# Two up-projection chunks in one tile, with 512-column products

## The chip, the cores and the metric

The kernel runs on one core of one Trainium2 chip. The metric is the device time of one execution in microseconds, as the median over runs; smaller is better. Beside it stands one profiled execution, whose span (first to last instruction of the program) is a little shorter than its time.

## The reference

One decoder layer on 256 tokens of width 1024, in float32:

```python
mix = hybrid_mixer(x, ...)                      # mLSTM branch and attention branch, gated, summed, projected
x = layer_norm(ALPHA * x + mix, ln1_g, ln1_b)
u = causal_dwconv(jnp.einsum("bsd,df->bsf", x, w_up), conv_ffn)     # w_up: 1024 x 5632
g, up = jnp.split(u, 2, axis=-1)
ffn = jnp.einsum("bsf,fd->bsd", jax.nn.silu(g) * up, w_down)        # w_down: 2816 x 1024
x = layer_norm(ALPHA * x + ffn, ln2_g, ln2_b)
```

The convolution is depthwise over three token positions. The change lies in the first columns of `w_up`.

## The kernel before, in words

Every float32 operand of a product is split into a high part (rounded to the matmul's float32r form) and a low part (the rest). A product of two such operands is three matmuls on TensorE, high by high, high by low and low by high, added up in PSUM (`mm3`, lines 125 to 127). The contraction over 1024 runs over eight slices of 128 rows (`KT` = 8, index k). One operand of a matmul is stationary (128 by 128, loaded before it), the other moves through (256 columns in nearly all of the kernel).

The weights come from HBM in a stream of 1 MB chunks in a fixed order (`chunk_order`): first projection, four groups of mixer projections, branch projections `wa` and `wb`, output projection `wo` (four chunks), and then up chunks (`up` 0 to 21) interleaved with down chunks (`dn`). One step of the main loop handles one chunk: it loads the chunk five places ahead (`load`, on the queue of SyncE), splits the chunk two places ahead into high and low parts (`split_parts`: a cast on ScalarE, line 91, and a subtraction on VectorE, line 92, in two halves), and then issues the step's matmuls (`step_up` and the like). Each engine runs its instructions in the order in which the program issues them.

An up chunk holds 128 columns of the gate half and 128 of the other half of `w_up`, so 256 columns. From chunk 2 on, the weights are stationary and all 256 tokens move (`mm_feat`), which gives features by tokens, as the convolution wants it. Chunks 0 and 1 are done the other way round (`mm_tok`): 128 tokens of the normalized activations are stationary and 256 weight columns move. So they can start on token half 0 while half 1 is still in the first layer norm. Their order is:

- step `up` 0: products of token half 0 for k = 0 to 6, both chunks at each k; four transposes of half 1 (`x1_transpose(1, 0)`, tile `ps_t`); products for k = 7; four more transposes of half 1; `x1_split` of both (tiles `x1h` and `x1l`);
- step `up` 1: products of token half 1, k = 0 to 7, both chunks at each k;
- then the results are copied to SBUF (`copy`, tile `tu`, on ScalarE), and transposed back in the middle of step `up` 2 (`back`, eight transposes, tile `ps_upT`).

Step `up` 2 takes its first stationary operand from a copy of it, `wfirst`. The split weights of chunks 0 and 1 do not lie in the stream's buffers but in four tiles of a pool of their own, `aheadh0`, `aheadl0`, `aheadh1` and `aheadl1`, filled during the steps `wo` 0 and `wo` 1.

Many tiles are allocated some words larger than needed, and used from an offset on. So the position in SBUF of a product's moving rows, relative to its stationary rows, is set by hand; the function `shift` does it for the stream's chunks:

```python
    if kind in ("vm", "vb", "o"):
        return 48
    if kind in ("wa", "wb"):
        return 56
    return 0 if kind in ("wo", "dn") else 16
```

The results of chunk j were accumulated in one PSUM bank per chunk (`ps_up`, 128 by 2 by 256: token half, column).

Of the kernel before, what the change touches and what calls it, by code (L numbers as in the profile page):

```python
# [11 lines left out]
F32R = mybir.dt.float32r  # L12
# [6 lines left out]
P = 128  # L19
S = 256  # L20
D = 1024
KT = D // P
# [47 lines left out]
class Kernel:  # L70
# [101 lines left out]
    def run(self):  # L172
# [28 lines left out]
        for part, a, b in (("x", 0, 1), ("w", 0, 1), ("x", 1, 4), ("w", 1, 2), ("w", 2, 4), ("x", 4, 8), ("w", 4, 6),  # L201
# [3 lines left out]
            else:  # L205
                s, c = cut[a][0], slice(cut[a][1].start, cut[b - 1][1].stop)
# [110 lines left out]
        first = {k: self.order.index((k, 0)) for k in ("wa", "wo", "up")}  # L317
        for s, (kind, i) in enumerate(self.order):
            if s == 8:
                self.elem_work(s, self.split_parts(s + 2))  # L320
                pre_cm.__exit__(None, None, None)
                self.open_att(att_cm.__enter__())
            if s == first["wa"]:
                self.elem_work(s)
                att_cm.__exit__(None, None, None)
                mix_cm.__exit__(None, None, None)
                self.open_post(post_cm.__enter__())
                mg = mg_cm.__enter__()
                self.mgh = mg.tile([P, KT, S], F32R, name="mgh")
                self.mgl = mg.tile([P, KT, S], F32R, name="mgl")  # L330
            if s == first["wo"]:
                self.elem_work(s)
                y_cm.__exit__(None, None, None)
                zp = ahead_cm.__enter__()
                for j in range(2):
                    self.extra[first["up"] + j] = tuple(
                        zp.tile([P, 2112], F32R, name=f"ahead{n}{j}")[:, 8:8 + 2048] for n in "hl")
            if s == first["up"]:
                self.elem_work(s)
                mg_cm.__exit__(None, None, None)  # L340
                self.fp = ffn_cm.__enter__()
            late = s == first["up"]
            self.elem_work(s, [] if late or s == 8 else self.split_parts(s + 2))
            self.load(s + 5)
            if s in (first["wo"], first["wo"] + 1):
                self.split(s + 4)
            getattr(self, "step_" + kind)(s, i, bo)
            for f in self.side_pe.pop(s, []):
                f()
            if late:  # L350

                self.wfirst = self.fp.tile([P, P + 64], F32R, name="wfirst")[:, 48:48 + P]
                nc.scalar.copy(self.wfirst, self.raw[s + 2][:, 0:P])
                self.split(s + 2)
# [602 lines left out]
    def step_up(self, s, i, *a):  # L957
        if i == 0:

            self.hid = {}  # L960
            self.pt_up = [self.ps_side([P, 2, S], f"ps_up{j}") for j in range(2)]
        if i < 2:
            for k in range(KT):
                if i == 0 and k == KT - 1:
                    self.x1_transpose(1, 0)
                for j in range(2):
                    self.mm_tok(self.w[s - i + j], [self.pt_up[j][:, t, :] for t in range(2)], self.x1h, self.x1l,
                                toks=(i,), ks=(k,))
            if i == 0:
                def trans():  # L970
                    self.x1_transpose(1, 1)
                    for h in range(2):
                        self.x1_split(1, h)
                self.side_pe.setdefault(s, []).append(trans)
                return
            del self.w[s - 1], self.w[s]
            tu = self.fp.tile([P, 2, 2, S], F32, name="tu")

            def copy():
                for j in range(2):  # L980
                    self.nc.scalar.copy(tu[:, j], self.pt_up[j])

            def back():
                for j in range(2):
                    ps = self.ps_side([P, 2, S], f"ps_upT{j}")
                    for f in range(2):
                        for t in range(2):
                            self.nc.tensor.transpose(ps[:, f, t * P:(t + 1) * P], tu[:, j, t, f * P:(f + 1) * P],
                                                     self.ident)
                    self.pt_up[j] = ps  # L990
            self.evac[s] = copy
            self.back = back
            self.up_parts = [self.up_evac(j, lambda j=j: self.pt_up[j]) for j in range(2)]
            return
        ps = self.ps_main(f"ps_up{i}")
        self.mm_feat(s, ps, self.x1h, self.x1l, *(self.back, self.wfirst) if i == 2 else ())
        conv, gate = self.up_evac(i, lambda: ps)
        parts = [conv, None, None, gate]
        if i == 2:
            (a0, b0), (a1, b1) = self.up_parts  # L1000
            parts = [a0, a1, conv, b0, None, None, b1, gate]
        self.evac[s] = parts
# [187 lines left out]
```

## Time and profile before

| | |
|---|---|
| median of 3 runs | 490.8 us (490.51 to 491.31) |
| profiled execution | 490.16 us, span 488.4 us |
| mean granted TensorE clock in it | 0.994 |
| TensorE busy | 477.0 us (98%) |
| VectorE busy | 369.3 us (76%) |
| ScalarE busy | 286.2 us (59%) |
| GpSimd busy | 30.6 us (6%) |
| moved by DMA | 93.77 MB, mean 192 GB/s |

A matmul's busy time counts it from start to modelled end, and successive matmuls overlap in the array. What TensorE gets through is therefore read from the starts of successive matmuls. "PEld" is the loading of the stationary operand, which goes on beside matmuls. The steps `up` 0 and `up` 1 run from 296.77 to 309.07 us of the span.

### The profile page before, as it was taken

To read this page: it belongs to the slowest core of one execution; us is meant where nothing else is said; L and a number is where in the kernel's file an instruction comes from. 1 tells how busy PE (TensorE), PEld (TensorE's weight loads), DVE (VectorE), ACT (ScalarE), POOL (GpSimd) and SP (SyncE) were. 2 spreads that over 40 slices of the span, in tenths; PEclk is the share of its full clock that TensorE was granted. 3 is DMA by queue.
4 is the path that set the end of the run, shared out by engine and by line. 5 is a ranking of instruction groups with operands and counts; after the bars stand their busy time and mean duration, and the time that the engine had idled before them with its cause. 6 is when DMAs were issued, how large, how long until landed. Compare 5 with 4: busy or idle time off the path is not lost.

```text
span 488.4 us, 9811 instructions
## 1 busy us (share of the span) xinstructions
PE 477.0 (98%) x4070; PEld 470.0 (96%) x4070; DVE 369.3 (76%) x659; ACT 286.2 (59%) x476; POOL 30.6 (6%) x46
## 2 busy tenths in 40 slices
PE   8999999999999999999999999999999999999992
PEld 4999999999999999999999999999999999999992
DVE  4967995788588858886677788988668766876886
ACT  5857767495658666856655622767456545654620
POOL 0600011001100110001000001000000000000001
PEclk9999999999999999999999999999999999999997
DMA  8984565555555645543964491827465556454202
GB/s 281 376 299 122 210 196 205 178 180 188 181 191 174 189 160 197 201 150 116 368 231 172 174 344 42 302 89 258 173 236 165 205 173 224 176 204 173 87 2 86
DMA packets 17886, 93.77 MB, mean 192 GB/s; under 512 B 4497, under 2 KB 4889, under 8 KB 7857
## 3 DMA queue, kind: packets, MB, share of 16 engines
q1 hardware_dynamic: 13682, 87.08, 50.1%
q0 software_dynamic: 4160, 6.07, 4.1%
q8 instruction: 32, 0.52, 0.4%
q14 instruction: 12, 0.10, 0.1%
HBM read 92.05 MB, written 2.63 MB: 194 GB/s over the span
## 4 chain that ended last, share of the span: by engine, by line
PE 97%; DMA 1%; DVE 1%; SPq 0%; ACT 0%; issue 0%; POOL 0%; POOLq 0%
PE ps_up L127 8%; PE ps_up L125 8%; PE ps_up L126 8%; PE ffn L127 4%; PE ffn L126 4%; PE ffn L125 4%; PE ps_vm L125 2%; PE ps_qm L125 2%; PE ps_vm L126 2%; PE ps_vm L127 2%; PE ps_ga L125 2%; PE ps_ga L127 2%; PE ps_vb L125 2%; PE ps_vb L126 2%; PE ps_vb L127 2%; PE ps_ga L126 2%
## 5 line engine op out<-in xcount | busy, mean ns | idle before, releaser
L92 DVE TENSOR_TENSOR wl<-raw,wh 128x1024 fp32r<-128x1024 f32 (+1 forms) x162 | 187.7, 1199 | 25.3 <-ACT wh L91 25.2
L91 ACT CAST wh<-raw 128x1024 fp32r<-128x1024 f32 (+1 forms) x162 | 158.4, 1030 | 8.6 <-DMA raw<-in_wst_dram 5.9
L127 PE MATMUL ps_up<-x1h,wl 128*128 128x256 f32 x320 | 88.5, 277 | 0.0
L126 PE MATMUL ps_up<-x1l,wh 128*128 128x256 f32 x320 | 88.5, 276 | 0.0
L125 PE MATMUL ps_up<-x1h,wh 128*128 128x256 f32 x319 | 88.3, 277 | 0.0
L126 PEld LDWEIGHTS ps_up<-x1l,wh 128*128 128x128 f32 x320 | 60.2, 188 | 0.0
L127 PEld LDWEIGHTS ps_up<-x1h,wl 128*128 128x128 f32 x320 | 60.1, 188 | 0.0
L125 PEld LDWEIGHTS ps_up<-x1h,wh 128*128 128x128 f32 x319 | 59.9, 188 | 0.0
L1020 DVE SCALAR_TENSOR_TENSOR cu<-ps_up,vec,cu 128x255 f32<-128x255 f32 (+1 forms) x80 | 33.1, 476 | 23.1 <-ACT cu L1016 23.0
L127 PE MATMUL ffn<-wh,hl 128*128 128x256 f32 (+1 forms) x170 | 47.7, 281 | 0.0
L126 PE MATMUL ffn<-wl,hh 128*128 128x256 f32 (+1 forms) x170 | 47.7, 281 | 0.0
L125 PE MATMUL ffn<-wh,hh 128*128 128x256 f32 (+1 forms) x170 | 47.7, 281 | 0.0
L91 ACT CAST hh<-cu 128x256 fp32r<-128x256 f32 x22 | 8.9, 407 | 42.9 <-DVE cu L1028 42.9
L126 PEld LDWEIGHTS ffn<-wl,hh 128*128 128x128 f32 x170 | 32.0, 188 | 0.3
L125 PEld LDWEIGHTS ffn<-wh,hh 128*128 128x128 f32 x170 | 31.9, 188 | 0.3
L127 PEld LDWEIGHTS ffn<-wh,hl 128*128 128x128 f32 x170 | 31.9, 188 | 0.3
L1016 ACT ACTIVATE cu<-ps_up,vec 128x256 f32<-128x256 f32 x40 | 16.7, 469 | 25.7 <-PE ps_up L127 25.7
L125 PE MATMUL ps_gb<-xth,wh 128*128 128x256 f32 x64 | 18.0, 282 | 0.0
L126 PE MATMUL ps_vm<-wl,xth 128*128 128x256 f32 x64 | 17.9, 280 | 0.0
L127 PE MATMUL ps_vm<-wh,xtl 128*128 128x256 f32 x64 | 17.9, 280 | 0.0
L927 POOL TENSOR_TENSOR rs<-rs,mhalf 128x1 f32<-128x1 f32 x4 | 2.7, 666 | 242.4 <-DVE rs L926 242.4
L125 PE MATMUL mix<-wh,mgh 128*128 128x256 f32 x64 | 17.8, 279 | 0.0
(295 smaller groups left out, 1441.7 us busy)
## 6 DMA issues: line engine op xcount, KB each, us to landing
raw<-in_wst_dram SPq DMA_DIRECT2D x78, 1024.0 KB, 4.9
raw<-in_wst_dram SPq DMA_DIRECT2D x5, 512.0 KB, 8.0
lnrow<-in_rows_dram POOLq DMA_DIRECT2D x4, 512.0 KB, 6.8
band<-table POOLq DMA_DIRECT2D x4, 384.0 KB, 12.2
toe<-band POOLq DMA_DIRECT2D x4, 256.0 KB, 4.4
xtok<-in_x_dram POOLq DMA_DIRECT2D x1, 1024.0 KB, 7.7
out_dram<-r SPq DMA_DIRECT2D x3, 256.0 KB, 2.0
raw<-in_wst_dram SPq DMA_DIRECT2D x2, 256.0 KB, 3.8
```

Source lines behind the costliest of these rows:

```text
L91: self.nc.scalar.copy(wh, raw)
L92: self.nc.vector.tensor_sub(wl, raw, wh.bitcast(F32))
L125: mm(ps, ah if first is None else first, bh, start=start, stop=False)
L126: mm(ps, ah, bl, start=False, stop=False)
L127: mm(ps, al, bh, start=False, stop=stop)
L927: nc.gpsimd.tensor_tensor(st["rs"], st["rs"], self.mhalf[:, 0:1], op=ALU.pow)
L1016: act.activation(cu[:, j, :], ps[:, j, :], AF.Copy, scale=tap(2, j))
L1020: v.scalar_tensor_tensor(cu[:, j, o:], ps[:, j, :S - o], tap(t, j), cu[:, j, o:], op0=ALU.mult, op1=ALU.add)
```

## The change

The four tiles become two, one of the high and one of the low parts, each with both chunks one behind the other. They are used from offset 24 words on instead of 8. At each k a token half's products take the columns of both chunks in one matmul: 512 columns, in two runs of 256 that lie 2048 words apart. The steps issue 48 matmuls of 512 columns instead of 96 of 256. A PSUM bank holds the results of one token half for both chunks instead of one chunk for both halves. The copies to `tu` go by token half accordingly; the layout of `tu` and the transposes behind it are as they were.

```diff
                 zp = ahead_cm.__enter__()
+                self.pair = [zp.tile([P, 4160], F32R, name="ahead" + n)[:, 24:24 + 4096] for n in "hl"]
                 for j in range(2):
-                    self.extra[first["up"] + j] = tuple(
-                        zp.tile([P, 2112], F32R, name=f"ahead{n}{j}")[:, 8:8 + 2048] for n in "hl")
+                    self.extra[first["up"] + j] = tuple(t[:, j * 2048:(j + 1) * 2048] for t in self.pair)
...
-            self.pt_up = [self.ps_side([P, 2, S], f"ps_up{j}") for j in range(2)]
+            self.pt_up = [self.ps_side([P, 2, S], f"ps_up0{t}") for t in range(2)]
         if i < 2:
+            wh, wl = (t.rearrange("p (j k f) -> p j k f", j=2, k=KT) for t in self.pair)
+            c = slice(i * P, (i + 1) * P)
             for k in range(KT):
                 if i == 0 and k == KT - 1:
                     self.x1_transpose(1, 0)
-                for j in range(2):
-                    self.mm_tok(self.w[s - i + j], [self.pt_up[j][:, t, :] for t in range(2)], self.x1h, self.x1l,
-                                toks=(i,), ks=(k,))
+                self.mm3(self.pt_up[i], self.x1h[:, k, c], self.x1l[:, k, c], wh[:, :, k, :], wl[:, :, k, :], k == 0,
+                         k == KT - 1)
...
             def copy():
-                for j in range(2):
-                    self.nc.scalar.copy(tu[:, j], self.pt_up[j])
+                for t in range(2):
+                    self.nc.scalar.copy(tu[:, :, t, :], self.pt_up[t])
```

## The prediction

> **What bounds the kernel now.** I read the page first, then the waits of the whole span, then the timelines of TensorE, ScalarE and VectorE around the changed steps.
>
> ```profile
> span 488.4 us, 9811 instructions
> PE 477.0 (98%) x4070; PEld 470.0 (96%) x4070; DVE 369.3 (76%) x659; ACT 286.2 (59%) x476; POOL 30.6 (6%) x46
> PE 97%; DMA 1%; DVE 1%; SPq 0%; ACT 0%; issue 0%; POOL 0%; POOLq 0%
> ```
>
> TensorE is busy 98% of the span, and the chain that ended last is 97% TensorE. The waits of TensorE are two of 1.2 us at the start, and one of its weight loads in the changed steps:
>
> ```profile
> PE ps_o L159 <- ACT wh L91: 1.2, 1, 1.2
> PE warm_ps L194 <- DVE warm L191: 1.2, 1, 1.2
> ...
> PEld ps_up L127 <- DVE x1l L92: 0.2, 1, 0.2
> ```
>
> So what the change is worth is what it does to the intervals between starts of products on TensorE, and nothing else. (A product's own duration in the trace, 276 ns, overlaps its successor's and is of no use.) The timeline of TensorE over the two changed steps, columns start and duration:
>
> ```profile
> 296.77 0.28 PE L125 MATMUL ps_up<-aheadh,x1h 128*128 128x256 f32 x1
> ...
> 301.60 0.28 PE L127 MATMUL ps_up<-aheadh,x1l 128*128 128x256 f32 x1
> 301.73 0.60 PE L947 MATMUL ps_t<-ident,x 128*128 128x128 f32 x4
> 302.08 0.37 PE L125 MATMUL ps_up<-aheadh,x1h 128*128 128x256 f32 x1
> ...
> 302.86 0.60 PE L947 MATMUL ps_t<-ident,x 128*128 128x128 f32 x4
> 303.21 0.36 PE L125 MATMUL ps_up<-aheadh,x1h 128*128 128x256 f32 x1
> 303.42 0.28 PE L126 MATMUL ps_up<-aheadl,x1h 128*128 128x256 f32 x1
> 303.73 0.39 PE L127 MATMUL ps_up<-aheadh,x1l 128*128 128x256 f32 x1
> ...
> 304.31 0.28 PE L125 MATMUL ps_up<-aheadh,x1h 128*128 128x256 f32 x1
> ...
> 309.07 0.28 PE L125 MATMUL ps_up<-x1h,wfirst 128*128 128x256 f32 x1
> ```
>
> The reader is to see two rhythms of the same instruction. Token half 0 has 42 products up to the first transposes: (301.73 − 296.77)/42 = 118 ns each. Half 1 has 42 from 304.31 on: (309.07 − 304.31)/42 = 113.3 ns each. It isn't the clock:
>
> ```profile
> core 0: us, PE busy (x), PEclk, DMA share, GB/s
> 296.77:301.73 4.96, 4.96 (x45) 1.00 0.02 3
> 304.31:309.07 4.76, 4.76 (x44) 1.00 0.54 177
> ```
>
> Full clock in both, and DMA nearly idle in the slower one. I call them the slow and the fast rhythm (+4.5 ns for each product).
>
> **What a 512-column product costs.** Two places have them: the first projection, and the first and last hidden chunk of the down projection.
>
> ```profile
> 9.27 0.39 PE L159 MATMUL ps_o<-wh,xth 128*128 128x512 f32 x1
> ...
> 17.20 0.39 PE L159 MATMUL ps_o0b<-wl,xth 128*128 128x512 f32 x1
> 321.25 0.39 PE L125 MATMUL ffn<-wh,hh 128*128 128x512 f32 x1
> ...
> 323.35 0.28 PE L125 MATMUL ffn<-wh,hh 128*128 128x256 f32 x1
> ```
>
> In the first, 35 intervals take 17.20 − 9.27 = 7.93 us: 226.6 ns, twice the fast 113.3. In the second, nine take 2.10 us: 233.3 ns. What differs in the program is the distance (first byte of the moving rows less first byte of the stationary rows, modulo 256). From the addresses that the allocator gives in the kernel before: in the first projection (43,072 − 95,296) it is 0; in `ffn`, and in nearly all 256-column products, 192. The changed steps have 192 now: 195,552 + 32 for `aheadh0`, less 119,872 for `x1h`. After, worked out by hand: two tiles of 16,640 bytes end where the four ended (229,344), so the rows begin at 196,064 + 96 = 196,160; less 119,872 that is 298 × 256, distance 0. For the low tile, 212,800, also 0. The text of the change holds, and I take 226.6; 233.3 is the upper end if distance isn't what parts the two places. The moving operand now has two runs of 256 columns 8 KB apart; no row has such an operand. Two separate products have two runs as well: 2 × 113.3 bounds it from below, no row of 512 columns being faster, and 2 × 118 from above. I take the lower end, which is what the contiguous 512 columns cost at this distance.
>
> The Trainium skill (TensorE: Matmul & The Clock Gate, Step-by-step: what each phase is for) gives TensorE two independent read ports, so that loading the next weights takes nothing from the running product. By that rule distance would not matter and the two places would show one interval; they show 226.6 and 233.3 ns, which speaks against it here, though the places differ in more than distance. By the rule the pair's 48 products would cost one interval between those two, whatever the pad, and the saving would lie between 0.20 and 0.52.
>
> **The change part by part.** The path now, from the rows above: 42 products 4.96; transposes 0.35; six products 0.78; transposes 0.35; six products with the wait 1.10; 42 products 4.76. Sum 12.30 us (296.77 to 309.07).
>
> After:
> - Half 0 before the transposes: 21 × 0.2266 = 4.76 (was 4.96). Saves 0.20.
> - First transposes 0.35: same instructions, if their input is there (below).
> - k = 7: three products, 0.68, and the 0.10 by which six now exceed 6 × 113.3 after a transpose: 0.78. Saves nothing.
> - Second transposes 0.35.
> - Half 1: 24 × 0.2266 = 5.44, and 0.10 for the restart: 5.54 (was 1.10 + 4.76 = 5.86). Saves 0.32, of which most is the wait for `x1l`.
> - Sum 11.78; saved 0.52 us. Bounds: at 233.3 ns each, 48 × 6.7 ns = 0.32 goes back, 0.20 left; at 2 × 118, 0.07 left.
>
> Do the inputs come early enough? The rows of VectorE and ScalarE, with idle time and what ended it:
>
> ```profile
> 301.51 0.87 DVE L935 SCALAR_TENSOR_TENSOR x<-r,rs,lnrow 128x256 f32<-128x256 f32 x2
> 302.98 0.69 DVE L92 TENSOR_TENSOR x1l<-ps_t,x1h 128x512 fp32r<-128x512 f32 x1 [0.60 <-ACT x1h L91]
> 305.26 4.63 DVE L92 TENSOR_TENSOR wl<-raw,wh 128x1024 fp32r<-128x1024 f32 x4 [0.46 <-ACT wh L91]
> 302.36 0.59 ACT L91 CAST x1h<-ps_t 128x512 fp32r<-128x512 f32 x1 [5.84 <-PE ps_t L947]
> 304.18 3.90 ACT L91 CAST wh<-raw 128x1024 fp32r<-128x1024 f32 x4
> 308.93 1.07 ACT L981 COPY tu<-ps_up 128x512 f32<-128x512 f32 x2 [0.85 <-PE ps_up L127]
> ```
>
> The second transposes read the last quarter of `x`, written at 301.51 + 0.87 = 302.38. They move from 302.86 to 302.66: cover 0.28 us; were it gone, the lateness would go onto TensorE one for one. The `x1l` of the wait comes from the first transposes through a cast and a subtraction; both engines are idle before (5.84 and 0.60 us), so the chain moves with the transposes, 0.20 earlier: `x1l` is done at 302.78 + 0.69 = 303.47. TensorE wants it after two products of half 1: 301.53 + 0.35 + 0.78 + 0.35 + 0.10 + 2 × 0.2266 = 303.56. Two products of 512 columns stand ahead of the first use of `x1l` where two of 256 stood; that is what takes the wait away. Spare 0.09 us, less the 0.06 from the subtraction's end to the product's start (303.67 to 303.73); between 0 and the old 0.2 may come back.
>
> The `tu` copies (ScalarE, 2 × 0.53): a copy now takes one token half, and half 0 is complete long before. Behind the four casts (end 308.08) one copy fits into the idle 0.85 us; the other follows half 1, whose end moves to 308.55, and ends about 309.5. Its reader, the first `ps_upT` transpose, would move from 311.90 to about 311.4: cover 1.9 us; a late copy would cost TensorE its lateness. The casts and subtractions that fill the pair are the same in number, size and queue, as are all DMAs; none is moved past another. The weights of the third up chunk are split by about 307.6 (305.26 + half of 4.63), needed at 308.55: cover 0.95. The 48 weight loads that fall away never end the chain: nothing. A VectorE or ScalarE wait added: none that I find.
>
> So span 487.9, profiled execution 490.16 − 0.52 = 489.64. The median of the runs shown is 490.8, 0.64 above the profiled one; from it, 490.3.
>
> **What is behind the pair.** A rhythm, once entered, holds until something breaks it:
>
> ```profile
> 311.90 1.04 PE L988 MATMUL ps_upT<-ident,tu 128*128 128x128 f32 x8
> 312.69 0.36 PE L125 MATMUL ps_up<-x1h,wh 128*128 128x256 f32 x1
> ...
> 315.60 0.28 PE L125 MATMUL ps_up<-x1h,wh 128*128 128x256 f32 x1
> ...
> 469.55 0.39 PE L125 MATMUL ffn<-wh,hh 128*128 128x512 f32 x1
> 470.95 0.28 PE L125 MATMUL ffn<-wh,hh 128*128 128x256 f32 x1
> 474.35 0.39 PE L125 MATMUL ffn<-wh,hh 128*128 128x512 f32 x1
> 475.05 0.28 PE L125 MATMUL ffn<-wh,hh 128*128 128x256 f32 x1
> ...
> 477.17 0.28 PE L125 MATMUL ffn<-wh,hh 128*128 128x256 f32 x1
> ```
>
> Up chunk 2 to its transposes, 309.07 to 311.90: 24 products at 118. Up chunk 3, 315.60 to 321.25: 48 at 118. Then nine 512-column products, and from 323.35 to 469.55 the fast rhythm without a break (146.2 us, 1,290 products, 113.3). Runs of 512 at distance 192: nine entered slow leave fast; six at 469.55, entered fast, leave fast (470.95 to 474.35, 30 products, 113.3); three at 474.35, entered fast, leave slow (475.05 to 477.17, 18 products, 118). An odd run turns the rhythm round, an even one keeps it. I forecast no change behind 309.07: after 512 columns at distance 0, at 17.20, the 256-column products run slow at once (17.43, 17.54, 17.66), and here chunk 2 is slow already.
>
> ```profile
> 17.43 0.28 PE L125 MATMUL ps_o<-wh,xth 128*128 128x256 f32 x1
> 17.54 0.28 PE L126 MATMUL ps_o<-wl,xth 128*128 128x256 f32 x1
> 17.66 0.28 PE L127 MATMUL ps_o<-wh,xtl 128*128 128x256 f32 x1
> ```
>
> **The rivals.**
> 1. Slower: chunks 2 and 3 become fast (−0.43 for 96 products), and the nine products, now entered fast, leave the rhythm slow for the 1,290 behind them: 1,290 × 4.5 ns = +5.8. Net with the pair: 490.3 − 0.43 + 5.8 = 495.7. It decides if the products from 312.69 on run at 113.3. For it: the odd-run rule. Against it: the eight `ps_upT` transposes stand between, and are untouched.
> 2. Faster: chunks 2 and 3 become fast and the nine still leave it fast: 489.9, on the edge of what counts as faster.
> 3. Distance does nothing: 512 columns cost the 233.3 of `ffn`: 490.6. Against it: 35 steady intervals at 226.6.
> 4. Each product has a fixed part which is now paid half as often. To reach 0.2% it would have to bring 0.46 us more, 9.6 ns below 226.6 for each of 48. Against it: 2 × 113.3 = 226.6, a fixed part of nil. Time: 489.8 or less. The Trainium skill (the same page, Back-to-back issue gap) has such a part, 2.5 ns on N/2.4, which makes 216 ns of 512 columns, by an estimate 0.5 us less than my sum; the trace's 226.6 does not agree.
>
> **How the numbers follow.** Forecast 0.68 (490.3; alone 490.1 to 490.7), rival 3 0.10, rival 1 0.09, rival 2 0.08, rival 4 0.03, an unseen late input 0.02. A measurement of this kernel tells about 0.2% (0.98 us) from no change; its runs spread from 490.51 to 491.31. Faster by that: rival 4, over half of rival 2, and 0.05 of the forecast for the scatter: 0.13. Slower: rival 1 and the late input: 0.11. Within: 0.76. The range reaches down to rival 4's edge, 489.6, and up past rival 3 by the scatter, 491.1; rival 1 lies outside.
>
> **What would show it.** 48 products of 128x512 in `ps_up`, 0.227 apart; 0.233 is rival 3. The distance from the first of them to the `wfirst` product: 11.8 us, not 12.30. No wait of a weight load for `x1l`; one of up to 0.2 means the cover was too thin. From 312.69 less 0.5 on, 118 ns; 113 is rival 1 or 2, and the interval after the nine `ffn` products tells which. The forecast is wrong if anything behind chunk 2 changes its rhythm, or the two-run operand costs more than two products.

## The result, and the profile after

The changed kernel takes 497.57 us (median of 4 runs, 497.12 to 498.84), the kernel before, on the same chip, 490.74 (4 runs, 490.51 to 491.31). The ratio is 1.0142, with a 95% interval of 1.013 to 1.0154: 6.8 us slower, where 0.5 us faster was forecast. The profiled execution of after is the longest of its four, 498.84 us.

The page of after: span, busy time of the engines, and the chain that ended last.

```profile
span 497.1 us, 9715 instructions
PE 485.3 (98%) x4022; PEld 475.0 (96%) x4022; DVE 370.1 (74%) x659; ACT 287.8 (58%) x476; POOL 30.5 (6%) x46
PE 97%; DMA 1%; DVE 1%; ACT 0%; POOL 0%; issue 0%; SPq 0%; POOLq 0%
```

Nothing here looks ill. TensorE has 48 instructions fewer and 8.3 us more of busy time, and it is still 97% of the chain. A kernel whose TensorE is busy 98% of the span can lose 7 us with no wait to show for it, because the loss is in the intervals between products. So the starts of products have to be read (columns: start, duration):

```profile
300.51 0.40 PE L125 MATMUL ps_up<-aheadh,x1h 128*128 128x512 f32 x1
...
305.31 0.60 PE L947 MATMUL ps_t<-ident,x 128*128 128x128 f32 x4
305.66 0.48 PE L125 MATMUL ps_up<-aheadh,x1h 128*128 128x512 f32 x1
306.44 0.60 PE L947 MATMUL ps_t<-ident,x 128*128 128x128 f32 x4
306.79 0.48 PE L125 MATMUL ps_up<-aheadh,x1h 128*128 128x512 f32 x1
307.11 0.40 PE L126 MATMUL ps_up<-aheadl,x1h 128*128 128x512 f32 x1
307.34 0.46 PE L127 MATMUL ps_up<-aheadh,x1l 128*128 128x512 f32 x1
307.64 0.39 PE L125 MATMUL ps_up<-aheadh,x1h 128*128 128x512 f32 x1
...
312.43 0.28 PE L125 MATMUL ps_up<-x1h,wfirst 128*128 128x256 f32 x1
315.15 1.03 PE L989 MATMUL ps_upT<-ident,tu 128*128 128x128 f32 x8
```

The pair runs from 300.51 to 312.43: 11.92 us, where it was 12.30. Then the stretches behind it, as windows of TensorE in after (columns: from and to, its length, TensorE's busy time and instructions, granted clock, DMA share, GB/s): up chunk 2 before the `ps_upT` transposes, up chunk 3, the nine 512-column products of the down projection, and the 1,290 products behind these:

```profile
312.43:315.15 2.72, 2.72 (x26) 1.00 0.87 355
318.76:324.20 5.44, 5.44 (x50) 1.00 0.35 148
324.20:326.29 2.09, 2.09 (x11) 1.00 0.00 0
326.29:478.22 151.93, 151.93 (x1291) 1.00 0.49 174
```

And the same four in before:

```profile
309.07:311.90 2.83, 2.83 (x27) 1.00 1.00 353
315.60:321.25 5.65, 5.65 (x50) 1.00 0.33 139
321.25:323.35 2.10, 2.10 (x12) 1.00 0.00 0
323.35:469.55 146.20, 146.20 (x1291) 1.00 0.51 181
```

The same 1,290 products take 151.93 instead of 146.20 us: 117.8 ns each instead of 113.3, at full clock in both. Chunk 3 went the other way, 5.44 for 48 products (113.3) where it had 5.65 (117.8). This is rival 1, to the sign of each part.

The rest of the loss lies ahead of the change, at the start of the kernel. The cast of the first weight piece, with its idle time and what ended it, and the first product of the first projection, in before:

```profile
3.98 0.62 ACT L91 CAST wh<-raw 128x512 fp32r<-128x512 f32 x1 [0.40 <-DMA raw<-in_wst_dram]
4.84 0.59 PE L159 MATMUL ps_o<-wh,xth 128*128 128x512 f32 x1
```

and in after:

```profile
6.60 0.62 ACT L91 CAST wh<-raw 128x512 fp32r<-128x512 f32 x1 [3.00 <-DMA raw<-in_wst_dram]
7.27 0.79 PE L159 MATMUL ps_o<-wh,xth 128*128 128x512 f32 x1 [1.57 <-ACT wh L91]
11.70 0.63 PE L159 MATMUL ps_o<-wl,xth 128*128 128x512 f32 x1
12.13 0.63 PE L159 MATMUL ps_o0b<-wl,xth 128*128 128x512 f32 x1
```

The first weight transfer lands 2.6 us later (6.60 − 3.98), TensorE idles 1.57 us, and then runs 512-column products at 0.43 us each, instead of 0.227, until 13.41 us. The Trainium skill (TensorE: Matmul & The Clock Gate, Wait — 56ns, not 53.3ns?) gives 426.7 ns for 512 columns while the array is cold; the 0.43 agrees. The profile gives 1.00 for the granted clock of that stretch, but this is no reading: the record of the clock in this trace begins only at 13.42 us. Where a record covers such a stretch, in the profile of the changed kernel with offset 8 (below), it shows 0.50 from 8.69 to 15.52 us, and the products there come at 0.43 us.

The account, of one profiled execution each: first up product 3.74 later (300.51 against 296.77); pair −0.38; chunks 2 and 3 −0.41 (12.18 to 11.77); the 1,290 products +5.73; the nine and the tail nothing. Sum 8.7, as the spans have it (497.1 − 488.4). The profiled execution is 1.3 us longer than the median of its four, and I take its start for the reason; the starts of the other three are not known. By the medians, 6.83 us, what is left for the start is 6.83 − 4.94 = 1.9 us (4.94 is 5.73 − 0.38 − 0.41).

### The profile page after: what moved, and what is told of

It reads as the page before. It is cut to its first block, busy times and chain, and to the rows that moved or that the text cites. A ratio compares the mean times of both kernels' runs of the same rounds, so it can differ in the third digit from the quotient of the medians.

```text
span 497.1 us, 9715 instructions
## 1 busy us (share of the span) xinstructions
PE 485.3 (98%) x4022; PEld 475.0 (96%) x4022; DVE 370.1 (74%) x659; ACT 287.8 (58%) x476; POOL 30.5 (6%) x46
## 4 chain that ended last, share of the span: by engine, by line
PE 97%; DMA 1%; DVE 1%; ACT 0%; POOL 0%; issue 0%; SPq 0%; POOLq 0%
PE ps_up L127 8%; PE ps_up L125 8%; PE ps_up L126 8%; PE ffn L127 4%; PE ffn L126 4%; PE ffn L125 4%; PE ps_vm L125 2%; PE ps_qm L125 2%; PE ps_vm L126 2%; PE ps_vm L127 2%; PE ps_ga L125 1%; PE ps_vb L125 1%; PE ps_ga L127 1%; PE ps_ga L126 1%; PE ps_vb L126 1%; PE ps_vb L127 1%
## 5 line engine op out<-in xcount | busy, mean ns | idle before, releaser
L127 PE MATMUL ps_up<-x1h,wl 128*128 128x256 f32 x320 | 89.9, 281 | 0.0
L126 PE MATMUL ps_up<-x1l,wh 128*128 128x256 f32 x320 | 89.9, 281 | 0.0
L125 PE MATMUL ps_up<-x1h,wh 128*128 128x256 f32 x319 | 89.7, 281 | 0.0
L126 PEld LDWEIGHTS ps_up<-x1l,wh 128*128 128x128 f32 x320 | 61.4, 192 | 0.0
```

Source lines behind the costliest of these rows:

```text
L125: mm(ps, ah if first is None else first, bh, start=start, stop=False)
L126: mm(ps, ah, bl, start=False, stop=False)
L127: mm(ps, al, bh, start=False, stop=stop)
```

## The experiments

Theory: the nine 512-column products turn the rhythm round, and the change altered the rhythm in which they are entered, so what is lost lies in the 1,290 products behind them; the start is a second, separate loss. Rivals: the long stretch is slow from something that the change moved itself (buffers, transfers, the late start), whatever the nine do; and, within the theory, that the width of the pair's products or their position in SBUF decides. The kernel before had medians of 491.14 (13 runs), 490.69 (24) and 490.95 (19) beside the first, second and third four.

**The changed kernel once more**, unaltered.

> The changed kernel, unaltered, once more. Of the 8.7 us by which its first profiled span was longer, the trace puts 5.6 on the rhythm of the 256-column products between the first and the last 512-column products of the down projection (117.8 ns instead of 113.3), and 3.7 on the start: the first weight piece landed late, TensorE's warm-up products ran out before it, and the first projection ran at half clock. Theory R (the rhythm is the effect of the change, the late start is chance): the rhythm is the same again, and the start may be either; without the late start the span is 488.4 - 0.39 - 0.41 + 0.12 + 5.60 + 0.13 - 0.15 = 493.3 us and the time about 495.1. Rival S (the start is late because of the change): the first up product starts near 300.5 us again, not near 296.8, and the time is 497.5.

497.42 us (4 runs, 497.19 to 498.16), ratio 1.0129 [1.0112, 1.0146]. The pair, chunks 2 and 3 (113.3) and the 1,290 products (117.8) are as in the first profile. The first product of the first projection comes at 7.42 us and the first up product at 299.18, 2.4 later than in before; the 495.1 that leaves the start out missed. The late start belongs to the kernel.

**The changed kernel, without the 512-column products of the first down chunk.**

```diff
-            n = cols[1] - cols[0] if k in (0, NF - 1) else 256
+            n = cols[1] - cols[0] if k == NF - 1 else 256
...
-                self.mm3(ps[:, o:o + n], hh, hl, w[0], w[1], k == 0, k == NF - 1)
+                self.mm3(ps[:, o:o + n], hh, hl, w[0], w[1], k == 0 and o == 0, k == NF - 1)
```

The second altered line gives the flag that starts a sum in PSUM only to the first of the products that take the place of one.

> The changed kernel with the first hidden chunk of the down projection in 256-column products, as the chunks behind it are (18 products instead of 9). Theory R (up chunks 2 and 3 are now fast, 113.3 ns, and it is the odd run of nine 512-column products behind them that turns the rhythm): nothing is left to turn it, the 1,290 products behind stay at 113.3, and against before the pair gives -0.39, chunks 2 and 3 -0.41, the nine products about -0.06: 490.7 - 0.9 = 489.9 us (up to 3.7 more if the start is late). Rival D (the slow rhythm comes from the changed pair itself, or from where its tiles lie, not from the nine products): the products behind stay at 117.8 ns and the time at 495 to 497.5.

491.58 us (10 runs), ratio 1.0017 [1.0002, 1.0032]. Chunk 3, and 1,260 products from up chunk 4 on, in windows with the columns of above:

```profile
317.20:322.64 5.44, 5.44 (x51) 1.00 0.35 146
328.13:470.93 142.80, 142.80 (x1262) 1.00 0.50 178
```

113.3 ns in both: entered fast, and nothing turns it round. The pair, the tiles and the late start (first up product at 298.94) are the changed kernel's, and 5.8 us are gone. This counts against anything in the pair itself, or in the start, that would slow the long stretch.

**The kernel before, with six 512-column products instead of nine** (the second token half's three go).

```diff
-            n = cols[1] - cols[0] if k in (0, NF - 1) else 256
+            n = cols[1] - cols[0] if k == NF - 1 or k == 0 and t == 0 else 256
...
-                self.mm3(ps[:, o:o + n], hh, hl, w[0], w[1], k == 0, k == NF - 1)
+                self.mm3(ps[:, o:o + n], hh, hl, w[0], w[1], k == 0 and o == 0, k == NF - 1)
```

> The kernel before, with the first hidden chunk of the down projection in 512 columns for token half 0 alone: six 512-column products in a row, then six of 256, instead of nine. Theory R with the parity rule (an odd run of 512-column products at distance 192 turns the rhythm round, an even one keeps it): chunks 2 and 3 enter it slow, as before, so the products behind it stay slow: 1,290 x 4.5 ns = 5.8 us, and the time is 496.5 us although the pair is as it was. Rival D, or a rule by which any run of 512 columns ends in the fast rhythm when entered slow: no change, 490.7 us.

497.1 us (4 runs), ratio 1.0124 [1.0109, 1.0139]; +5.96. Chunk 3 and the same 1,260 products:

```profile
316.70:322.35 5.65, 5.65 (x50) 1.00 0.36 148
327.99:476.39 148.40, 148.40 (x1263) 1.00 0.49 171
```

Nothing of the pair is touched, and the whole loss is there: six, entered slow, leave slow. The same six, entered fast, come in the changed kernel:

```diff
-            n = cols[1] - cols[0] if k in (0, NF - 1) else 256
+            n = cols[1] - cols[0] if k == NF - 1 or k == 0 and t == 0 else 256
...
-                self.mm3(ps[:, o:o + n], hh, hl, w[0], w[1], k == 0, k == NF - 1)
+                self.mm3(ps[:, o:o + n], hh, hl, w[0], w[1], k == 0 and o == 0, k == NF - 1)
```

> The changed kernel with the first hidden chunk of the down projection in 512 columns for token half 0 alone: six 512-column products instead of nine, entered fast. Theory R with the even-run rule (six entered fast left fast at 469.55 us of the kernel before): the 1,290 products behind are fast, the time is that of e2, 491.6 us. Rival (any run of 512 columns at distance 192 leaves the rhythm slow when entered fast, as three and nine did): 497.4 us.

491.32 us (10 runs), ratio 1.0014 [1.0004, 1.0023]: 142.80 us for the 1,260 products, with the late start still there (first product at 7.25 us). Together with the kernels before and after this makes all four cases: nine slow to fast, nine fast to slow, six slow to slow, six fast to fast.

**What sets the rhythm in which the nine are entered.** First the tiles' offset in the changed kernel, 24 words to 8 (distance 192 instead of 0):

```diff
-                self.pair = [zp.tile([P, 4160], F32R, name="ahead" + n)[:, 24:24 + 4096] for n in "hl"]
+                self.pair = [zp.tile([P, 4160], F32R, name="ahead" + n)[:, 8:8 + 4096] for n in "hl"]
```

> The changed kernel with the pair's rows from offset 8 words on instead of 24, so that the 512-column products run at distance 192 as in the down projection, instead of 0. Expected of the pair: 48 products at 233.3 instead of 226.6 ns, +0.32 us. Behind it theory R allows two outcomes only: chunk 2 entered slow (then the nine products leave the rhythm fast, 113.3 ns, and the time is about 490.7 - 0.39 + 0.32 = 490.6) or entered fast (then slow behind, 117.8 ns, about 495.5 and up to 3.7 more with a late start). By the even-run rule, with the first products after a transpose in the slow pattern, slow in chunk 2 is the likelier. Rival D (the 512-column pair itself slows what follows, at any distance): slow behind, 495.5 or more, with chunk 2 in either rhythm.

498.12 us (4 runs), ratio 1.0149 [1.0125, 1.0174]. The pair's products take 233 ns on average (231 and 236 in turn), so distance does set their price. Chunk 2 behind the transposes and chunk 3 are slow again, as in before, so position sets the entry too. But the nine then left it slow:

```profile
320.00:325.65 5.65, 5.65 (x51) 1.00 0.33 139
331.28:479.68 148.40, 148.40 (x1262) 1.00 0.48 171
```

The odd-run rule fails here. Their intervals were 236, 236, 231, 236, 230, 236, 231, 236, 231 ns. Elsewhere nine entered slow begin with 231, 229, 236, and nine entered fast go 226, 236, 230, 236, 231, 236, 231, 236, 230: but for its first interval this run has the order of those entered fast. "Slow" and "fast" of the 256-column products are thus not the whole state that a run of 512 sees; what shifted it stays open. The traces hold a closer reading than odd and even. Past its start such a run alternates between about 231 and 236 ns. In 33 of the 34 runs of 512 in the down projections of all profiles, this one among them, a run whose last interval is 235 to 236 leaves fast, and one with 230 or 231 leaves slow. That is read from the traces; no run tests it by itself.

Next the changed kernel with its tiles and offset, but two products of 256 columns in place of each of 512:

```diff
-                self.mm3(self.pt_up[i], self.x1h[:, k, c], self.x1l[:, k, c], wh[:, :, k, :], wl[:, :, k, :], k == 0,
-                         k == KT - 1)
+                for j in range(2):
+                    self.mm3(self.pt_up[i][:, j, :], self.x1h[:, k, c], self.x1l[:, k, c], wh[:, j, k, :], wl[:, j, k, :],
+                             k == 0 and j == 0, k == KT - 1 and j == 1)
```

> The changed kernel with its pair tile and offset (distance 0), but products of 256 columns as before, each chunk's own: the layout of the change alone, without the 512 columns. Of the pair: 96 products at distance 0, between 113.3 and 123 ns (the few single products at other distances): 12.2 to 13.1 us instead of 12.3. Behind it theory R allows only two times, by the rhythm in which chunk 3 ends: slow, and the nine products then leave it fast (490.5 to 491.6, plus 1.3 if the start is late), or fast, and they leave it slow (495.5 to 497.4). It tells whether the 512 columns or the place of the rows turned chunk 2 fast: by the 512 columns, chunk 2 is slow here; by the place, it is fast.

496.28 us (4 runs), ratio 1.0116 [1.0103, 1.013]. Of the pair each product takes 120.0 ns, a third rhythm. Chunk 2 is slow before the transposes (117.8) and fast behind them, chunk 3 fast, and the 1,260 slow (148.40 us). So the width of 512 isn't needed for the loss. The offset of 24 alone is enough for it, as the kernel before shows with one number altered in its four tiles (it isn't needed either, since offset 8 in the changed kernel lost as much):

```diff
-                        zp.tile([P, 2112], F32R, name=f"ahead{n}{j}")[:, 8:8 + 2048] for n in "hl")
+                        zp.tile([P, 2112], F32R, name=f"ahead{n}{j}")[:, 24:24 + 2048] for n in "hl")
```

> The kernel before with one number altered: the four ahead tiles are used from offset 24 words on instead of 8, so that the pair's 256-column products run at distance 0, as in e7. Theory R with the place of the rows as the cause: as e7, chunk 3 is fast after its transposes and the nine products leave 1,290 products slow: pair 12.7 us instead of 12.3, time 496.3. Rival M (merging the tiles, not their offset, turned the rhythm in e7): chunk 3 slow, 1,290 products fast, time 490.7 + 0.4 = 491.1.

496.47 us (4 runs), ratio 1.0115 [1.0099, 1.0131]: +5.5 us from 64 bytes. Chunk 2 up to the transposes, chunk 3, the 1,260 products:

```profile
310.20:313.02 2.82, 2.82 (x26) 1.00 0.91 381
316.63:322.07 5.44, 5.44 (x50) 1.00 0.36 152
327.70:476.10 148.40, 148.40 (x1263) 1.00 0.49 171
```

The rhythm changes over the transposes: 24 products at 117.8 ahead of them, 113.3 behind. With offset 40 (distance 64) in the changed kernel:

```diff
-                self.pair = [zp.tile([P, 4160], F32R, name="ahead" + n)[:, 24:24 + 4096] for n in "hl"]
+                self.pair = [zp.tile([P, 4160], F32R, name="ahead" + n)[:, 40:40 + 4096] for n in "hl"]
```

> The changed kernel with the pair's rows from offset 40 words on instead of 24: 512 columns at distance 64. Chunk 3 was fast with offset 24 (after, e7) and slow with offset 8 (before, e4), whatever the rhythm of chunk 2 ahead of the transposes. No theory says which it is here. If the rhythm behind the pair were decided by the offset in an orderly way, a further offset would tell how; if it is a matter of the exact time at which the transposes end, either comes out. By theory R the time has two values: 490.3 plus 1.3 for the late start where the 1,290 products are fast, 496.2 plus 1.3 where they are slow, each plus 0 to 0.4 for the pair at this distance.

Ten runs fall into two groups, 492.0 to 492.28 (4) and 496.68 to 497.38 (6); median 496.78, ratio 1.0085 [1.0051, 1.0119] over both. The profiled one is of the first group: pair at 229 ns on average, chunks 2 and 3 slow, the nine leave it fast (142.80 us). The other group, 5 us longer, was not profiled; that its nine left it slow is likely from its size, and only argued.

**No 512-column product in the down projection at all**, with the changed pair.

```diff
-            n = cols[1] - cols[0] if k in (0, NF - 1) else 256
+            n = 256
...
-                self.mm3(ps[:, o:o + n], hh, hl, w[0], w[1], k == 0, k == NF - 1)
+                self.mm3(ps[:, o:o + n], hh, hl, w[0], w[1], k == 0 and o == 0, k == NF - 1 and c + n == cols[1])
```

> The changed kernel with the whole down projection in 256-column products, first and last hidden chunk too. Theory R: nothing turns the rhythm from up chunk 2 to the end, so the last 36 products, slow in e2 and in the kernel before, are fast as well (36 x 4.5 = 0.16 us), and nine products of 512 columns at 232 ns become 18 at 113.3 (0.05): 0.2 us under e2. With the start of e2 that is 491.4 us beside 491.1 for the kernel before; with the start of the kernel before, 490.0. Rival D (any slow rhythm comes back without a 512-column run): the tail stays at 117.8 ns and nothing is saved there.

489.54 us (8 runs, 488.84 to 490.14), ratio 0.9974 [0.9964, 0.9984]: faster than both kernels. The page's line of engines and the two windows:

```profile
PE 476.3 (98%) x4040; PEld 467.7 (96%) x4040; DVE 369.3 (76%) x659; ACT 286.2 (59%) x476; POOL 31.4 (6%) x46
315.27:320.71 5.44, 5.44 (x50) 1.00 0.46 175
326.19:468.99 142.80, 142.80 (x1262) 1.00 0.50 178
```

But for a few products at transposes and at one late input, the products from chunk 2 to the end come at 113.3 ns. It is 2.0 us under the kernel that still had its tail of 512. Of this the tail explains about 0.2 (9.41 us from the first product of the last hidden chunk to the last product, where it was 9.62), and the start most of the rest: it is early (first product at 5.01, first up product at 297.01, where it was 298.94). The kernel before with 256 columns throughout was not run, so how much of the 0.9974 is owed to the pair is not shown.

**The start.** That kernel has 18 matmul instructions more than the changed one. If their number decides the start, unused ones will do. Thirty transposes whose result nobody reads, behind the last product of the kernel just shown:

```diff
+        pad = self.ps_main("pad").rearrange("p a b -> p (a b)")
+        for _ in range(30):
+            self.nc.tensor.transpose(pad[:, 0:P], self.x1[:, 0, 0:P], self.ident)
```

> As e5, with 30 more TensorE transposes after the last product, beside the last layer norm, whose output is not used: the number of TensorE's matmuls and weight loads is again that of the kernel before (4,070 each). It tests the start: in four profiles of kernels with the pair the first weight piece landed about 6.5 us after the span's start and DMA packets between 3 and 6 us took 290 to 550 ns, in two profiles without the pair it landed near 4 to 5 us and they took 117 to 174 ns. Theory P (the start depends on where the shorter or longer program lets the data lie in memory, and follows the instruction count): the first projection starts near 4.8 to 5.3 us again, and the time is 1.3 us under e5, 490.0. Rival N (the start has nothing to do with the count of instructions): start and time as in e5, 491.4. Should the extra transposes lie in the way of the end: up to 1 us more.

489.74 us (11 runs), ratio 0.9979 [0.997, 0.9988]; early start (5.13), so nothing told apart, its base being early too. Eighteen of them behind the changed kernel:

```diff
...
+        for _ in range(18):
...
```

> The changed kernel with 18 unused TensorE transposes after the last product: 4,040 matmuls; nothing else is altered. Theory P: the start is early, and what is left is the rhythm: 497.5 - 1.3 = 496.2 us, with the 1,290 products at 117.8 ns as in the changed kernel. Rival N: 497.5.

495.6 us (4 runs, 495.49 to 496.55), ratio 1.0097 [1.008, 1.0114]. The rows of the start:

```profile
4.28 0.62 ACT L91 CAST wh<-raw 128x512 fp32r<-128x512 f32 x1 [0.67 <-DMA raw<-in_wst_dram]
5.10 0.58 PE L159 MATMUL ps_o<-wh,xth 128*128 128x512 f32 x1
```

Work added at the end of the kernel makes its first transfer land 2.3 us earlier, and the kernel 1.9 us shorter. What remains over before, 495.6 − 490.95 = 4.65 us, is near the 4.94 of the account without the start. In all profiles of these kernels the first projection began at 7.1 to 7.4 us where there were 4,031 matmuls or fewer (six profiles), and at 4.8 to 5.4 us where there were 4,040 or more (eight). Late and early starts came on each of the three chips that the experiments ran on, so the chip does not decide it. From 3 to 6 us the DMA engines moved 98 to 118 GB/s in the six late profiles and 221 to 258 in the eight early ones, so all transfers were slower then, and not the first weight transfer alone. Why the length of the program matters to them no run shows.

The last one adds nine such transposes (4,040) to the kernel without the first down chunk's 512.

```diff
...
+        for _ in range(9):
...
```

> The kernel of e2 with nine unused TensorE transposes after the last product, beside the last layer norm: 4,040 matmuls, as e5 has. So far the start was late in every profile of a kernel with at most 4,031 matmuls (after, e1, e2, e4, e8) and early in every one with 4,040 or more (before, e3, e5, e6, e7). Theory P (the length of the program decides the start, by where it lets instructions or data lie): first projection near 5 us instead of 7.2, and the time about 1.3 us under e2's 491.6, so 490.3. Rival N (it was something else that e5 changed in the down projection): late, 491.6.

The start is early (5.35), as expected. Of ten runs seven took 489.76 to 491.18 and three 495.88, 495.93 and 497.43; median 490.34, ratio 1.0009 [0.9977, 1.0042]. The profiled one took 495.93, and its timeline shows how (VectorE and TensorE, start, duration, idle time and what ended it):

```profile
323.74 0.43 DVE L92 TENSOR_TENSOR hl<-cu,hh 128x256 fp32r<-128x256 f32 x1 [0.47 <-ACT hh L91]
324.19 0.28 PE L126 MATMUL ffn<-wl,hh 128*128 128x256 f32 x1
324.30 0.30 PE L127 MATMUL ffn<-wh,hl 128*128 128x256 f32 x1
324.44 0.28 PE L125 MATMUL ffn<-wh,hh 128*128 128x256 f32 x1
324.56 0.28 PE L126 MATMUL ffn<-wl,hh 128*128 128x256 f32 x1
324.67 0.28 PE L127 MATMUL ffn<-wh,hl 128*128 128x256 f32 x1
```

The first product that reads `hl` starts at 324.30; `hl` is written until 324.17. The next product follows it 135 ns later instead of 113, and from there on the products come at 117.8 to the end of the stretch. A delay of 22 ns cost some 5.8 us (495.9 against 490.1); that `hl`, only just in time, made it is inferred from the place. The kernel without the nine transposes has one of 32 ns in the same place and is back at 113.3 by chunk 4, so a delay can turn the rhythm round and need not. This profile also has the second exception to the odd-run rule: the six products of 512 at 475.31, entered slow, take 233 to 234 ns each without alternating, and leave fast.

## Why the prediction was wrong, step by step

- **48 products at 226.6 ns, distance 0.** Right: 226.7 once settled, 229 on average at distance 64, 233 at 192. By the Trainium skill (TensorE: Matmul & The Clock Gate, Step-by-step: what each phase is for), with its two independent read ports, loading the next weights takes nothing from the running product, which gives no reason for such a difference. With the product, the width and the program alike and only the offset altered, these runs show one.
- **The pair, 0.52 saved.** 0.38 measured. Half 0 took 4.80 for 4.76; half 1 took 5.64 for 5.54.
- **No wait for `x1l`.** Wrong by a little: the estimated spare of 0.03 us was none, and the weight load still waited for it.

```profile
307.31 0.19 PEld L127 LDWEIGHTS ps_up<-aheadh,x1l 128*128 128x128 f32 x1 [0.24 <-DVE x1l L92]
```

  It cost the interval from 307.34 to 307.64, 0.30 instead of 0.23, which is most of half 1's excess.
- **The `tu` copies are covered.** Right: the second ends at 313.21, its reader starts at 315.15.

```profile
312.62 0.59 ACT L982 COPY tu<-ps_up 128x512 f32<-128x512 f32 x1 [0.49 <-PE ps_up L127]
```

- **"I forecast no change behind 309.07."** This is the step that failed. It stood on one analogue, the 256-column products that ran slow at 17.43 behind 512 columns at distance 0, and on chunk 2 having been slow already. In after, chunk 2 runs at 113.3 from its first product, ahead of the transposes. The argument that they stand between was no protection: they pass a fast rhythm on (after) or change it (slow to fast with offset 24 in before's tiles, fast to slow with offset 8 in the changed one).
- **Rival 1, +5.8 and chances of 0.09.** Its size was right (5.73) and so was its condition, the products behind the transposes at 113.3. The weight was wrong. The odd-run rule was read from three runs of 512 in one execution. It holds in 32 of the 34 of all profiles, so given the entry it mostly settles what happens; nothing in the profile told the entry, so the entry deserved something near even chances rather than a forecast.
- **The start.** No rival had it: 1.9 us of the 6.8. 490.74 + 4.94 + the 1.9 that the eighteen transposes gave back is 497.6, against 497.57 measured.

Open: what sets the rhythm over the transposes, why nine entered slow left slow with offset 8 and six entered slow left fast in the last profile, and why the program's length moves the first transfer.

## What to carry to other kernels

Where TensorE is busy throughout and one instruction has two rhythms, price an edit by the rhythm that it leaves behind it (products behind times the difference, here 1,290 × 4.5 ns), not by the stretch edited (0.4 us). Find what turns the rhythm round, and take that out first: here the nine 512-column products of the first down chunk spare nine matmul instructions and decide over 5.7 us; with uniform 256 columns behind it, the changed kernel is at 0.9974 of before. Time such a kernel in several executions, since it can fall into either rhythm from one to the next.

## What the runs showed of the hardware

- The same float32r product of 256 columns has at least three steady intervals at full granted clock, 113.3, 117.8 and 120.0 ns. The first two were each held for over a thousand products, the third for 42 in a row, with its operands at distance 0.
- 64 bytes in the position of four weight tiles cost 5.5 us, nearly all of it in products that do not touch these tiles.
- A run of 512-column products in the down projection alternates between about 231 and 236 ns, and its last interval tells the rhythm of the 256-column products behind it (33 of 34 runs).
- Behind one product that came 22 ns late, the next 151 us ran in the slow rhythm; that the delay made it is inferred from the place. Two of the kernels run in two groups, 5 to 6 us apart.
- Eighteen unused transposes at the end of the program moved the landing of the first transfer by 2.3 us, and the whole time by 1.9 us.
